# Splitting the opening's weights and norming its embeddings on another engine, and moving the S5 rotations' multiples

## The chip, the cores and the metric

The kernel runs on one core of a Trainium2 chip. The metric is the device time of one execution in microseconds (us), as the median of several runs. The core has five engines with instruction queues of their own: TensorE (PE, with its weight loads shown as PEld), VectorE (DVE), ScalarE (ACT), GpSimd (POOL) and SyncE (SP, which here only issues DMAs). Each engine works through its queue in order, and semaphores make one engine wait for another.

## The reference, cut to what matters

One decoder layer over 1024 tokens of width 1024, with a memory of 256 tokens:

```
h     = layer_norm(x); mem_n = layer_norm(mem)
z     = h @ w_in                        # columns: u (512) | q k | v | r (512) | gate rank 16
y_ssm = s5_mixer(u)                     # 32 groups x 16 channels, 64 complex states a group
y_gla = gla_mixer(q, k, v, r, gates)    # 4 heads, gated linear attention
h     = layer_norm(a*h + concat(y_ssm, y_gla) @ w_out)
h     = layer_norm(a*h + cross_attention(h, mem_n, w_mq, w_mkv, w_mo))
h     = layer_norm(a*h + relu(h @ w_ff1)**2 @ w_ff2)
```

In the S5 mixer each state obeys s[l] = A s[l-1] + (B u)[l] with a complex A = mag (cos + i sin) for each of the 2048 states, and y = Re(C s) + D u. The gate r enters as r * sigmoid(r).

## The kernel before, in words

**Products.** Everything is in float32. For a matmul that must keep that accuracy, each operand is *split* into a high part (rounded by ScalarE as it copies, `act(hi, src)`) and a low part (`lo = src - hi`, one tensor_tensor on VectorE or GpSimd, line 150); `mm3` then issues three matmuls (high x high, high x low, low x high, line 171). `weight` loads a raw block of 128x1024 into one of four `raw` buffers by SyncE's queue and splits it into one of five buffers (`hl`). Which engine makes the low part is given block by block by a bit mask: `eng(bits, i)` is VectorE where bit i is set, and GpSimd where it isn't. The masks that the change touches are `MO0` (the output weights `wo` of memory head 0), `MWR` (the four blocks `wr` of the gate r) and `MWU` (the four blocks `wu` of the S5 input u).

**The opening.** Memory is normed and head 0 of the cross-attention is folded into weights (`mem_stream`: its products with `kvT`, the split projection of the memory). Then the eight embedding tiles of 128 tokens follow. `embed(tk)` norms tile `tk` in place (`layer_norm`, tile `xs`), has TensorE transpose it (line 259), splits the transposed tile into `h0T`, and `z_block` multiplies the tile before it by `wr`; `r_epi` finishes the gate (tile `rt`). In `layer_norm` the tile's mean and variance come from VectorE (`bn_stats`, and a chain of one-element instructions on `tq`). Then there are two ways, chosen tile by tile by a bit of `LIGHT`:

```
if light:
    stt(V, xt[:, lo_], xt[:, lo_], mv[:, 0:1], rows[:, 0, lo_], ALU.subtract, ALU.mult)
    stt(V, tq[:, 3:4], mv[:, 0:1], -1.0, tq[:, 0:1], ALU.mult, ALU.mult)
    act(xt[:, hi_], xt[:, hi_], AF.Identity, scale=tq[:, 0:1], bias=tq[:, 3:4])
    tt(G, xt[:, hi_], xt[:, hi_], rows[:, 0, hi_], ALU.mult)
else:
    stt(V, xt, xt, mv[:, 0:1], rows[:, 0, :], ALU.subtract, ALU.mult)
    act(xt[:, hi_], xt[:, hi_], scale=tq[:, 0:1])
```

After either, VectorE scales and shifts the lower half and GpSimd adds the shift of the upper half. So in the light way VectorE handles only the lower 512 columns, and GpSimd has two passes over the upper ones. `LIGHT` = 191 makes all tiles but tile 6 light.

**S5's tables.** VectorE works out exp, sin and cos of the 2048 states' steps (tiles of 128x16 in `prm`), the powers 0 to 8 of A (`pw`, in `par`), and the *rotations' multiples* `E0` and `E1`: powers of exp(8i angle) from which a batch's rotations over 128 blocks of eight tokens are put together. Sixteen pairs of groups are handled in eight batches of two. `s5_t0(b)` builds a batch's tables by outer products on VectorE: `Vt` (C times the powers), the input weights `wtmp` (B times the powers), and the rotations `rot` (E0 times E1). `s5_t1` transposes the weights, `s5_t2` makes the taps `Mt` by way of a DMA, `s5_m1` loads the inputs, `s5_m2` runs the scan on the rotated products, and `s5_m3` makes the outputs.

**What sets the order.** The program traces its instructions in source order, and a planner lays out each engine's queue ahead of time from that order and its own estimates of when operands are ready; earlier source lines have priority among those ready. `behind(split_u)` opens a stretch of the source (closed by `order.close()`) whose VectorE instructions may not be issued ahead of `split_u`, the last VectorE split of `wu`. The rotations' multiples stand ahead of that stretch, while the rest of the tables, the masks of the GLA levels and the first `s5_t0` stand in it. After it, `z_stream` multiplies by `wu`, with the four decay gates (`gate`, tiles `gst`, stored by SyncE's queue, line 559) between its products, and later S5 batches are interleaved with the rest.

Of the kernel before, what the change touches and what calls it, by code (L numbers as in the profile page):

```python
# [9 lines left out]
I32 = mybir.dt.int32  # L10
U8 = mybir.dt.uint8
AF = mybir.ActivationFunctionType
ALU = mybir.AluOpType
# [4 lines left out]
P = 128  # L18
# [5 lines left out]
NJ = NG // 2  # L24
# [5 lines left out]
LEVELS = (1, 2, 4, 8, 16, 32, 64)  # L30
# [2 lines left out]
FA = 2.6  # L33
FB = 4
FT = 4
LIGHT = 191
MT = 64
ML = 15
GE = 2.6
GA = 8.0  # L40
MW = 3
MV0 = 3
MO0 = 2
MWR = 4
MWU = 7
MQK = 3
MVV = 11
MW1 = 3
# [33 lines left out]
def hybrid_layer(  # L82
# [9 lines left out]
    V = nc.vector  # L92
    A = nc.scalar
    G = nc.gpsimd
# [20 lines left out]
    const = ctx.enter_context(tc.tile_pool(name="const", bufs=1))  # L115
# [27 lines left out]
    def ts(e, o, i, s1, s2=None, op0=ALU.mult, op1=None):  # L143
        if s2 is None:
            e.tensor_scalar(out=o, in0=i, scalar1=s1, scalar2=None, op0=op0)
        else:
            e.tensor_scalar(out=o, in0=i, scalar1=s1, scalar2=s2, op0=op0, op1=op1)  # L147

    def tt(e, o, a, b, op):
        e.tensor_tensor(out=o, in0=a, in1=b, op=op)  # L150

    def stt(e, o, a, s, b, op0, op1):
        e.scalar_tensor_tensor(out=o, in0=a, scalar=s, in1=b, op0=op0, op1=op1)  # L153
# [28 lines left out]
    def rsqrt_n(y, v, eps, t):  # L182
# [5 lines left out]
        for _ in range(3):  # L188
# [7 lines left out]
                    pattern=[[-1, P]], channel_multiplier=1)  # L196

    def eng(bits, i):
        return V if bits >> i & 1 else G
# [67 lines left out]
    prm_s = slot("prm", [P, 4096])  # L267
# [20 lines left out]
    for b in range(4):  # L288
        z = (b + 1) % 3 * 512 + 512
        t = mrow[:, 0:2, :].rearrange("p a n -> p (a n)")[:, z:z + 512].rearrange("p (k m) -> p k m", k=2)  # L290
# [94 lines left out]
    def mem_stream(heads, tag, room=None):  # L385
        nxt = mem_load(heads[0])
        yield 0
        for h in heads:
# [7 lines left out]
            for r0 in range(0, D, 256):  # L396
                ps = bank("d", (P, 2, MEM))
                for c in range(2):
                    ck = r0 // P + c
                    for dk in range(2):  # L400
# [7 lines left out]
            wo = [weight(w_mo[h * 256:(h + 1) * 256, n * 512:(n + 1) * 512].rearrange("(k p) n -> p k n", p=P),  # L408
                         [P, 2, 512], eng(MO1 if room is None else MO0, n), None if room is None else room[:, n]) for n in range(2)]
            vT = yield from mem_proj(ws)  # L410
# [66 lines left out]
    def embed(tk):  # L477
        xt = xs[tk // 4][:, tk % 4, :]
        layer_norm(xt, rows, LIGHT >> tk & 1)
        transposes(lambda k: xt[:, k * P:(k + 1) * P],  # L480
# [29 lines left out]
    def pt(n=1):  # L510
        i = scr_n[0]
        scr_n[0] += n
        return scr[:, i, :] if n == 1 else scr[:, i:i + n, :]

    e = V
    prm = pt(6)
    lr, li, ls = prm[:, 0, :], prm[:, 2, :], prm[:, 4, :]
# [49 lines left out]
    def keep(*dims):  # L567
        n = 1
        for d in dims:
            n *= d  # L570
        o = par_n[0]
        par_n[0] += n
        names = "abcd"[:len(dims)]
        return par[:, o:o + n].rearrange("p (" + " ".join(names) + ") -> p " + " ".join(names),
                                         **dict(zip(names, dims)))
# [34 lines left out]
    def cmul(e, o_re, o_im, a_re, a_im, b_re, b_im, t):  # L610
        tt(e, o_re, a_re, b_re, ALU.mult)
        tt(e, t, a_im, b_im, ALU.mult)
        tt(e, o_re, o_re, t, ALU.subtract)
        tt(e, o_im, a_re, b_im, ALU.mult)
        tt(e, t, a_im, b_re, ALU.mult)
        tt(e, o_im, o_im, t, ALU.add)
# [5 lines left out]
    mag, mag1 = exp_parts(zre)  # L622

    kk, hh, x2, sn, cm1, cs = (pt() for _ in range(6))
# [24 lines left out]
    tw = pt(4)  # L649
# [4 lines left out]
    n = 1  # L654
    while n < 8:
        bc = [pw[:, r, n, :].unsqueeze(1).to_broadcast([P, n, NJ]) for r in range(2)]
# [1 line left out]
             pw[:, 0, 1:n + 1, :], pw[:, 1, 1:n + 1, :], bc[0], bc[1], tw[:, 0:n, :])  # L658
        n *= 2

    m8 = keep(NJ)
    tt(e, m8, mag, mag, ALU.mult)
    tt(e, m8, m8, m8, ALU.mult)
    tt(e, m8, m8, m8, ALU.mult)
    pr, pi_ = cs, sn
    for i in range(3):
        o = (pt(), pt())
        cmul(e, o[0], o[1], pr, pi_, pr, pi_, tw[:, 0, :])
        pr, pi_ = o
    E0 = keep(2, 16, NJ)  # L670
    E1 = keep(2, 8, NJ)
    te = pt(8)
    for Et, cnt in ((E0, 16), (E1, 8)):
        G.memset(Et[:, 0, 0, :], 1.0)
        G.memset(Et[:, 1, 0, :], 0.0)
        n = 1
        while n < cnt:
            bc = [z.unsqueeze(1).to_broadcast([P, n, NJ]) for z in (pr, pi_)]
            cmul(e, Et[:, 0, n:2 * n, :], Et[:, 1, n:2 * n, :], Et[:, 0, 0:n, :], Et[:, 1, 0:n, :],
                 bc[0], bc[1], te[:, 0:n, :])  # L680
            o = (pt(), pt())
            cmul(e, o[0], o[1], pr, pi_, pr, pi_, tw[:, 0, :])
            pr, pi_ = o
            n *= 2

    order = ExitStack()
    order.enter_context(behind(split_u))

# [21 lines left out]
         fim.unsqueeze(2).to_broadcast([P, NJ, SH]), b2[:, 2])  # L710


    mask = const.tile([P, 5, 64], U8, name="mask")
    mk = prm_s[:, 0:5 * P].rearrange("p (a t) -> p a t", a=5)
    ii, jj, xf, gt, ge = (mk[:, i, :] for i in range(5))
    ii, jj = ii.bitcast(I32), jj.bitcast(I32)
    G.iota(ii, pattern=[[1, P]], base=0, channel_multiplier=0)
    G.iota(jj, pattern=[[0, P]], base=0, channel_multiplier=1)
    tt(V, gt, ii, jj, ALU.is_gt)
    tt(V, ii, ii, jj, ALU.bitwise_xor)  # L720
    tt(V, xf, ii, gt, ALU.mult)

    def right(ap, s, two):
        return ap.rearrange("p (n w s) -> p n w s", w=2, s=s)[:, :, two, :]

    for li, s in enumerate(LEVELS[:5]):
        ts(V, ge, xf, float(s), op0=ALU.is_ge)
        stt(V, mask[:, li, :].rearrange("p (n s) -> p n s", s=s), right(xf, s, 1), float(2 * s),
            right(ge, s, 1), ALU.is_lt, ALU.mult)


    NB = 2

    class Batch:


        def __init__(self, bt):
            self.bt = bt
            sa = slot("s5", [P, 4096])

            def region(o, pat, **kw):
                n = 1
                for v in kw.values():
                    n *= v
                return sa[:, o:o + n].rearrange(pat, **kw)

            self.uT = region(0, "p (g c) -> p g c", g=2 * NB, c=P)
            self.Mt = region(512, "p (g j n) -> p g j n", j=NB, g=2, n=P)
            self.Wt = region(1024, "p (r j n) -> p r j n", r=2, j=NB, n=P)
            self.wtmp = region(1536, "p (r j n) -> p r j n", r=2, j=NB, n=P)  # L750
            self.S = region(1024, "p (r j c) -> p r j c", r=2, j=NB, c=P)
            self.rot = region(2048, "p (r j c) -> p r j c", r=2, j=NB, c=P)
            self.rs = region(2560, "p (r j c) -> p r j c", r=2, j=NB, c=P)
            self.Vt = region(3072, "p (r j t h) -> p r j t h", r=2, j=NB, t=9, h=SH)
            self.tmp = region(3648, "p (j c) -> p j c", j=NB, c=P)
            self.tmp9 = region(0, "p (r j t h) -> p r j t h", r=2, j=NB, t=9, h=SH)

    rows2 = [slice(0, 64), slice(64, 128)]


    def s5_t0(b):

        j0 = b.bt * NB
        js = slice(j0, j0 + NB)
        def outer(e, o, w, a, m, shape, signs):

            shape = [P] + shape
            for r in range(2):
                for q in range(2):
                    tt(e, (o, w)[r][:, q], a(q ^ r).to_broadcast(shape), m(r).to_broadcast(shape), ALU.mult)  # L770
            for q in range(2):
                if signs[q]:
                    tt(e, o[:, q], o[:, q], w[:, q], signs[q])
                else:
                    stt(e, o[:, q], o[:, q], -1.0, w[:, q], ALU.mult, ALU.subtract)


        outer(V, b.Vt, b.tmp9, lambda q: C2[:, q, js, :].unsqueeze(2),
              lambda r: pw[:, r, :, js].rearrange("p t j -> p j t").unsqueeze(3), [NB, 9, SH], (ALU.subtract, None))

        w_, t_ = (z.rearrange("p r j (t h) -> p r j t h", t=T) for z in (b.wtmp, b.rs))
        outer(V, w_, t_, lambda q: Bb[:, q, js, :].unsqueeze(2),
              lambda r: pw[:, r, 0:8, js].rearrange("p t j -> p j t")[:, :, ::-1].unsqueeze(3), [NB, T, SH],
              (ALU.subtract, ALU.add))

        w_, t_ = (z.rearrange("p r j (a b) -> p r j a b", a=8) for z in (b.rot, b.S))
        outer(eng(CM, b.bt), w_, t_, lambda q: E0[:, q, :, js].rearrange("p a j -> p j a").unsqueeze(2),
              lambda r: E1[:, r, :, js].rearrange("p a j -> p j a").unsqueeze(3), [NB, 8, 16], (ALU.subtract, ALU.add))

# [88 lines left out]
    bat = {}  # L878

    def s5(stage_, i):  # L880
        if i < NBT:
            if stage_ is s5_t0:
                bat[i] = Batch(i)
            stage_(bat[i])

    s5(s5_t0, 0)
    order.close()


    qk = slot("qk", [P, 4, SEQ])  # L890
# [79 lines left out]
    dc, o = {}, 0  # L970
    for s in LEVELS + (P,):
        w = 2 * SEQ // s
# [444 lines left out]
    for _ in range(2):  # L1417
        z = wp.tile([P, 2, 2, 512], F32R, tag="w", name="w1q")
# [271 lines left out]
    for k in range(6):  # L1690
        banks = [(m, 0, 512, bank(("ddds", "ssgg")[k % 2][m])) for m in range(4)]
        for gp in range(NP):
            s = k * NP + gp
# [19 lines left out]
    for ms in ((0, 1), (2,), (3,)):  # L1713
        parts = [(m, c, w) for m in ms for c, w in (((0, 256), (256, 256)) if m == 3 else ((0, 512),))]
        for part in ([parts] if len(ms) == 2 else [[z] for z in parts]):
            banks = [(m, c, w, bank("d")[:, 0:w]) for m, c, w in part]
            for gp in range(NP):
                s = 6 * NP + gp
# [4 lines left out]
            for m, c, w, po in banks:  # L1723
                r = res(4 + m)[:, c:c + w]
# [38 lines left out]
```

## Time and profile before

| | |
|---|---|
| median of 3 runs | 1375.15 us (1372.4 to 1378.64) |
| the profiled execution | 1375.71 us, its span 1373.9 us |
| granted TensorE clock, mean | 0.992 of full speed |
| busy: TensorE / VectorE / ScalarE / GpSimd | 1332.4 / 962.5 / 572.7 / 367.3 us |
| DMA | 199.82 MB, mean 145 GB/s |

The span runs from the first to the last instruction of the core. A row of the profile names start and duration (in a timeline), engine, line of the kernel, operation, what is written and read, the shape and how often; in brackets stands how long the engine had been idle before it, and what ended that. Where several equal instructions follow each other they are one row with a count. A busy share is a mean over stages with different limits, so the opening is read by itself.

### The profile page before, as it was taken

How to read it: one execution, taken by the hardware profiler on the slowest of the kernel's cores; microseconds unless marked ns; L12 is line 12 of the kernel's file. 1: busy time of each engine (PE TensorE's matmuls, PEld its weight loads, DVE VectorE, ACT ScalarE, POOL GpSimd, SP SyncE). 2: the span in 40 equal slices, each digit the busy share in tenths (PEclk: the TensorE clock that was granted, in tenths of full speed). 3: DMA queues.
4: the chain of work that ended last, by engine and by line, in shares of the span. 5: the costliest groups of instructions: out<-in, count | busy, mean ns of one | idle time of the engine just before them, and what ended most of it. 6: DMA issues, size and time to landing. Idle time of an engine off the chain costs nothing. (4 is left out here: it accounts for less than half of the span.)

```text
span 1373.9 us, 18798 instructions
## 1 busy us (share of the span) xinstructions
PE 1332.4 (97%) x6824; PEld 1106.7 (81%) x6824; DVE 962.5 (70%) x1751; ACT 572.7 (42%) x953; POOL 367.3 (27%) x269
## 2 busy tenths in 40 slices
PE   6789999999999999999999999999999999999997
PEld 6576788888998888888888788788887888888886
DVE  8999788756874379745379866665556576668784
ACT  4434433342554244333023754545456343344441
POOL 1552010211534123000013134343332243003353
PEclk9899999999999999999999999999999999999999
DMA  9832342543667120311112557644446994334432
GB/s 301 267 125 85 112 123 53 176 152 118 219 197 248 53 86 16 123 31 31 32 46 85 185 171 242 197 155 162 155 167 228 318 318 132 103 108 159 136 108 92
DMA packets 155514, 199.82 MB, mean 145 GB/s; under 512 B 16294, under 2 KB 86044, under 8 KB 155292
## 3 DMA queue, kind: packets, MB, share of 16 engines
q1 hardware_dynamic: 143536, 179.44, 40.1%
q10 hardware_dynamic: 11884, 19.17, 3.8%
q8 instruction: 54, 0.88, 0.3%
q14 instruction: 40, 0.33, 0.1%
HBM read 140.38 MB, written 58.20 MB: 145 GB/s over the span
## 5 line engine op out<-in xcount | busy, mean ns | idle before, releaser
L171 PE MATMUL ps_d<-xt,w1q 128*128 128x512 f32 x576 | 137.4, 389 | 0.7 <-DVE hid L150 0.7
L171 PEld LDWEIGHTS ps_d<-xt,w1q 128*128 128x128 f32 x576 | 108.1, 188 | 23.5 <-DVE hid L150 1.1
L171 PE MATMUL ps_s<-cell 128*128 128x512 f32 x432 | 113.0, 389 | 0.0
L171 PE MATMUL ps_d<-cell 128*128 128x512 f32 x432 | 106.0, 389 | 0.5 <-DVE hid L150 0.5
L150 POOL TENSOR_TENSOR R<-R,row 128x512 f32<-128x512 f32 x27 | 35.6, 1332 | 231.9 <-ACT R L156 225.3
L171 PEld LDWEIGHTS ps_d<-cell 128*128 128x128 f32 x432 | 81.0, 188 | 17.7 <-DVE hid L150 0.9
L171 PEld LDWEIGHTS ps_s<-cell 128*128 128x128 f32 x432 | 81.1, 188 | 16.8
L156 ACT ACTIVATE hl<-raw 128x1024 fp32r<-128x1024 f32 x62 | 65.2, 1059 | 68.9 <-PE ps_d L171 57.6
L171 PE MATMUL ps_d<-hl,y 128*128 128x512 f32 x384 | 92.6, 395 | 0.0
L171 PE MATMUL ps_g<-xb,w1q 128*128 128x512 f32 x384 | 92.1, 392 | 0.0
L171 PE MATMUL ps_d<-hl,h0T 128*128 128x512 f32 x384 | 91.0, 393 | 0.6 <-DVE h0T L150 0.6
L171 PE MATMUL ps_d<-h0T,hl 128*128 128x512 f32 x384 | 90.8, 393 | 0.8 <-DVE hl L150 0.8
L171 PE MATMUL ps_d<-hl,p 128*128 128x512 f32 x384 | 89.0, 391 | 0.0
L171 PEld LDWEIGHTS ps_d<-h0T,hl 128*128 128x128 f32 x384 | 71.1, 188 | 20.1 <-issue 2.2
L156 ACT ACTIVATE hid<-hid 128x512 f32<-128x512 f32 x112 | 70.8, 632 | 39.2 <-DVE hid L150 37.4
L150 DVE TENSOR_TENSOR hl<-raw,hl 128x1024 fp32r<-128x1024 f32 x53 | 70.3, 1339 | 21.8 <-ACT hl L156 21.3
L150 DVE TENSOR_TENSOR cell<-ha,cell 128x1024 fp32r<-128x1024 f32 x56 | 82.3, 1471 | 3.5 <-ACT cell L156 3.5
L171 PEld LDWEIGHTS ps_d<-hl,h0T 128*128 128x128 f32 x384 | 71.1, 188 | 16.2 <-DVE h0T L150 1.1
L171 PEld LDWEIGHTS ps_d<-hl,p 128*128 128x128 f32 x384 | 71.6, 188 | 14.6
L171 PEld LDWEIGHTS ps_g<-xb,w1q 128*128 128x128 f32 x384 | 71.5, 188 | 14.6
L171 PEld LDWEIGHTS ps_d<-hl,y 128*128 128x128 f32 x384 | 70.7, 188 | 14.6 <-issue 0.3
L156 ACT ACTIVATE w1q<-raw 128x512 fp32r<-128x512 f32 x80 | 50.1, 629 | 69.0 <-PE ps_d L171 27.3
(295 smaller groups left out, 2744.9 us busy)
## 6 DMA issues: line engine op xcount, KB each, us to landing
g_d<-hid SPq DMA_DIRECT2D x112, 256.0 KB
ha<-g_d SPq DMA_DIRECT2D x56, 512.0 KB
raw<-in_w_ff_dram SPq DMA_DIRECT2D x40, 512.0 KB
b<-in_w_ff_dram SPq DMA_DIRECT2D x32, 512.0 KB
raw<-in_w_mkv_dram SPq DMA_DIRECT2D x16, 512.0 KB
raw<-in_w_in_dram SPq DMA_DIRECT2D x16, 512.0 KB
wq<-in_w_mq_dram SPq DMA_DIRECT2D x8, 512.0 KB
xs<-in_x_dram SPq DMA_DIRECT2D x8, 512.0 KB
```

Source lines behind the costliest of these rows:

```text
L150: e.tensor_tensor(out=o, in0=a, in1=b, op=op)
L156: A.activation(out=o, in_=i, func=f, **kw)
L171: PE.matmul(o, lhs(i), rhs(j), start=first and n == 0, stop=last and n == 2, skip_group_check=more)
```

## The change

- `LIGHT` becomes 0: all eight embedding tiles take the other way of norming. VectorE subtracts the mean and multiplies by the gain over all 1024 columns, and GpSimd keeps one pass over the upper half.
- `MO0` 2 to 3, `MWR` 4 to 15, `MWU` 7 to 15: five low parts (one block of `wo`, three of `wr`, one of `wu`) go from GpSimd to VectorE. `split_u` is then the split of the last block of `wu`.
- The code that makes `m8`, `E0` and `E1` moves from ahead of the stretch behind `split_u` to its end, after the first `s5_t0`. The first batch's rotations are made after it, by a new function `s5_r0`; the later batches call it at the end of `s5_t0`. Its scratch moves from the place of the states `S` to a new region `rt`, which is the place of the taps `Mt`.
- The masks move behind `order.close()`.

```
-LIGHT = 191        -MO0 = 2     -MWR = 4      -MWU = 7
+LIGHT = 0          +MO0 = 3     +MWR = 15     +MWU = 15
...
-    m8 = keep(NJ)
-    tt(e, m8, mag, mag, ALU.mult)
...                                   # E0, E1: moved, see below
     order = ExitStack()
     order.enter_context(behind(split_u))
...
-    mask = const.tile([P, 5, 64], U8, name="mask")
...
+            self.rt = region(512, "p (r j c) -> p r j c", r=2, j=NB, c=P)
...
     def s5_t0(b):
...
-        w_, t_ = (z.rearrange("p r j (a b) -> p r j a b", a=8) for z in (b.rot, b.S))
+        if b.bt:
+            s5_r0(b)
+
+    def s5_r0(b):
+        js = slice(b.bt * NB, b.bt * NB + NB)
+        w_, t_ = (z.rearrange("p r j (a b) -> p r j a b", a=8) for z in (b.rot, b.rt))
         outer(eng(CM, b.bt), w_, t_, lambda q: E0[:, q, :, js].rearrange("p a j -> p j a").unsqueeze(2),
               lambda r: E1[:, r, :, js].rearrange("p a j -> p j a").unsqueeze(3), [NB, 8, 16], (ALU.subtract, ALU.add))
...
     s5(s5_t0, 0)
+    m8 = keep(NJ)
+    tt(e, m8, mag, mag, ALU.mult)
+    tt(e, m8, m8, m8, ALU.mult)
+    tt(e, m8, m8, m8, ALU.mult)
+    pr, pi_ = cs, sn
+    for i in range(3):
+        o = (pt(), pt())
+        cmul(e, o[0], o[1], pr, pi_, pr, pi_, tw[:, 0, :])
+        pr, pi_ = o
+    E0 = keep(2, 16, NJ)
+    E1 = keep(2, 8, NJ)
+    te = pt(8)
+    for Et, cnt in ((E0, 16), (E1, 8)):
+        G.memset(Et[:, 0, 0, :], 1.0)
+        G.memset(Et[:, 1, 0, :], 0.0)
+        n = 1
+        while n < cnt:
+            bc = [z.unsqueeze(1).to_broadcast([P, n, NJ]) for z in (pr, pi_)]
+            cmul(e, Et[:, 0, n:2 * n, :], Et[:, 1, n:2 * n, :], Et[:, 0, 0:n, :], Et[:, 1, 0:n, :],
+                 bc[0], bc[1], te[:, 0:n, :])
+            o = (pt(), pt())
+            cmul(e, o[0], o[1], pr, pi_, pr, pi_, tw[:, 0, :])
+            pr, pi_ = o
+            n *= 2
+    s5_r0(bat[0])
     order.close()
+    mask = const.tile([P, 5, 64], U8, name="mask")
...
```

`cmul` is six VectorE instructions.

More of the change, by code (lines that the diff above doesn't have):

```diff
@@ L35 @@
 FT = 4
-LIGHT = 191
+LIGHT = 0
 MT = 64
@@ L42 @@
 MV0 = 3
-MO0 = 2
-MWR = 4
-MWU = 7
+MO0 = 3
+MWR = 15
+MWU = 15
 MQK = 3
@@ L659, in hybrid_layer @@
         n *= 2
-    m8 = keep(NJ)
-    tt(e, m8, mag, mag, ALU.mult)
[L663 to L684, printed above, removed]
     order = ExitStack()
@@ L710, in hybrid_layer @@
          fim.unsqueeze(2).to_broadcast([P, NJ, SH]), b2[:, 2])
-    mask = const.tile([P, 5, 64], U8, name="mask")
[L714 to L729, printed above, removed]
     NB = 2
@@ L758, in hybrid_layer, with outer @@
     rows2 = [slice(0, 64), slice(64, 128)]
+    def outer(e, o, w, a, m, shape, signs):
+        shape = [P] + shape
+        for r in range(2):
+            for q in range(2):
+                tt(e, (o, w)[r][:, q], a(q ^ r).to_broadcast(shape), m(r).to_broadcast(shape), ALU.mult)
+        for q in range(2):
+            if signs[q]:
+                tt(e, o[:, q], o[:, q], w[:, q], signs[q])
+            else:
+                stt(e, o[:, q], o[:, q], -1.0, w[:, q], ALU.mult, ALU.subtract)
     def s5_t0(b):
@@ L764, in s5_t0 @@
         js = slice(j0, j0 + NB)
[L765 to L775, printed above, removed]
         outer(V, b.Vt, b.tmp9, lambda q: C2[:, q, js, :].unsqueeze(2),
@@ L886, in hybrid_layer, with right @@
     s5(s5_t0, 0)
-    order.close()
+    m8 = keep(NJ)
[23 more added lines that the diff above has]
+    s5_r0(bat[0])
+    order.close()
+    mask = const.tile([P, 5, 64], U8, name="mask")
+    mk = prm_s[:, 0:5 * P].rearrange("p (a t) -> p a t", a=5)
+    ii, jj, xf, gt, ge = (mk[:, i, :] for i in range(5))
+    ii, jj = ii.bitcast(I32), jj.bitcast(I32)
+    G.iota(ii, pattern=[[1, P]], base=0, channel_multiplier=0)
+    G.iota(jj, pattern=[[0, P]], base=0, channel_multiplier=1)
+    tt(V, gt, ii, jj, ALU.is_gt)
+    tt(V, ii, ii, jj, ALU.bitwise_xor)
+    tt(V, xf, ii, gt, ALU.mult)
+    def right(ap, s, two):
+        return ap.rearrange("p (n w s) -> p n w s", w=2, s=s)[:, :, two, :]
+    for li, s in enumerate(LEVELS[:5]):
+        ts(V, ge, xf, float(s), op0=ALU.is_ge)
+        stt(V, mask[:, li, :].rearrange("p (n s) -> p n s", s=s), right(xf, s, 1), float(2 * s),
+            right(ge, s, 1), ALU.is_lt, ALU.mult)
     qk = slot("qk", [P, 4, SEQ])
```

## The prediction

> **What bounds the kernel now.** I read the page first, then the table of stretches, then TensorE's waits in the opening, then each engine's order in time there.
>
> ```profile
> PE 1332.4 (97%) x6824; PEld 1106.7 (81%) x6824; DVE 962.5 (70%) x1751; ACT 572.7 (42%) x953; POOL 367.3 (27%) x269
> ```
>
> ```profile
> 0.00:122.50 122.50, 97.24 (x537) 78.67 (x537) 113.81 (x379) 50.68 (x81) 48.19 (x51) 0.96 0.60 203
> 122.50:314.00 191.50, 191.45 (x1094) 151.69 (x1094) 147.00 (x334) 76.38 (x126) 24.96 (x36) 1.00 0.41 127
> ```
>
> The columns of the stretches are: length, then busy time of PE, PEld, DVE, ACT and POOL, then granted clock, DMA share and GB/s. TensorE is idle for 1373.9 - 1332.4 = 41.5 us in all. 25.3 us of that (122.5 - 97.24) lies in the opening, which holds nearly all that the change touches, and 0.05 us in the next 191.5 us. So a microsecond that TensorE's queue gains by 122.5 us moves everything behind it by a microsecond, and more than the opening's waits can't be won. From 20 us on these are, by the chain of waits (total, times, longest):
>
> ```profile
> PE ps_d L171 <- DVE kvT L150: 5.3, 2, 5.0
> PE ps_s L259 <- POOL xs L150: 4.7, 4, 2.3
> PE ps_d L171 <- ACT kvT L156: 3.4, 1, 3.4
> PE ps_d L171 <- DVE hl L150: 0.8, 1, 0.8
> PE ps_d L171 <- DVE h0T L150: 0.6, 1, 0.6
> ```
>
> That is 14.8 us: two waits for the split of head 0's value projection (kvT), four for GpSimd's part of the embedding norm, one for a split of the S5 input weights (hl). VectorE is busy 113.81 of 122.5 us, so most of these are its queue being late. Part of this busy time is waiting:
>
> ```profile
> 30.14 2.40 POOL L150 TENSOR_TENSOR wo<-raw,wo 128x1024 fp32r<-128x1024 f32 x1 [23.71 <-ACT wo L156]
> 36.76 5.87 POOL L150 TENSOR_TENSOR hl<-raw,hl 128x1024 fp32r<-128x1024 f32 x2 [4.22 <-DMA prm<-in_w_gate_up_dram]
> ```
>
> ```profile
> 30.18 2.38 DVE L153 SCALAR_TENSOR_TENSOR tq<-tq 128x1 f32<-128x1 f32 x1
> ...
> 37.05 3.37 DVE L150 TENSOR_TENSOR wo<-raw,wo 128x1024 fp32r<-128x1024 f32 x1
> 40.34 2.32 DVE L153 SCALAR_TENSOR_TENSOR tq<-tq 128x1 f32<-128x1 f32 x1
> ```
>
> The instruction of one element per row at 30.18 ends at 32.56, when GpSimd's weight split (30.14 to 32.54) ends. The one at 40.34 ends at 42.66, with GpSimd's pair (36.76 to 42.63). A weight split by GpSimd takes 2.4 us and holds VectorE up for nearly as long. VectorE does one in 1.23 us:
>
> ```profile
> 27.45 1.23 DVE L150 TENSOR_TENSOR hl<-raw,hl 128x1024 fp32r<-128x1024 f32 x1 [1.45 <-ACT hl L156]
> ```
>
> **The change part by part.** *Five weight splits go to VectorE* (head 0's first output weight, three of the gate's, the last of S5's). Each adds 1.23 us, 6.2 us in all. Beside the stalls above stand these under the fourth and the fifth split:
>
> ```profile
> 55.48 2.46 DVE L145 TENSOR_SCALAR prm<-prm 128x16 f32<-128x16 f32 x2
> ...
> 117.88 4.56 DVE L150 TENSOR_TENSOR hl<-raw,hl 128x1024 fp32r<-128x1024 f32 x2
> ```
>
> The small instructions of the norms that no GpSimd pass meets:
>
> ```profile
> L153 DVE SCALAR_TENSOR_TENSOR tq<-mv,tq 128x1 f32<-128x1 f32 x7 | 1.0, 148 | 0.0
> ```
>
> At 0.15 us for such a one, 30.18 loses 2.2, 40.34 loses 2.2, 37.05 loses 3.37 - 1.23 = 2.1, 55.48 loses 2.2, and 117.88 loses 4.56 - 2.46 = 2.1: 10.8 us less. Of it 6.5 us less and, with three splits, 3.7 us more lie ahead of this:
>
> ```profile
> 45.67 0.68 DVE L150 TENSOR_TENSOR kvT<-ps_d,kvT 128x512 fp32r<-128x512 f32 x1
> ```
>
> The weight buffers are also let go earlier. SyncE holds a gate weight's load for the buffer of the split at 30.14 (3.4 us), and ScalarE then waits 0.69 us for that weight, directly ahead of its half of kvT:
>
> ```profile
> SPq L205 <- POOL wo L150: 3.4, 1, 3.4
> ```
>
> ```profile
> 38.31 1.06 ACT L156 ACTIVATE hl<-raw 128x1024 fp32r<-128x1024 f32 x1 [0.69 <-DMA raw<-in_w_in_dram]
> ```
>
> I take 0.6 us of that off the 3.4 us wait.
>
> *Seven embedding tiles go the other way of norming*: one VectorE pass over 1024 in place of a pass over 512 and a small one, and one GpSimd pass in place of two.
>
> ```profile
> L150 POOL TENSOR_TENSOR xs<-xs,row 128x512 f32<-128x512 f32 x15 | 22.9, 1529 | 7.4 <-ACT xs L156 6.8
> ```
>
> ```profile
> L153 DVE SCALAR_TENSOR_TENSOR tq<-tq 128x1 f32<-128x1 f32 x48 | 18.4, 402 | 0.2
> ...
> L153 DVE SCALAR_TENSOR_TENSOR xs<-xs,mv,row 128x1024 f32<-128x1024 f32 x1 | 1.3, 1267 | 0.0
> ```
>
> ```profile
> L153 DVE SCALAR_TENSOR_TENSOR xs<-xs,mv,row x8: 731/743/1729, 21.3 to 86.8; 128x512 f32<-128x512 f32 x7, 128x1024 f32<-128x1024 f32 x1
> ```
>
> VectorE pays 1.27 - 0.74 - 0.15 = 0.38 us a tile, 2.6 us in all (0.74 is the median of the eight, the last row). GpSimd loses 7 x 1.53 = 10.7 us. The 48 small instructions cost 18.4 us where 48 x 0.15 = 7.2 would do: 11.2 us of stalls, 4.4 of them the two under splits above. The passes over 512, 0.74 at the median and up to 1.73, add an estimated 3 us. So some 10 us lie under GpSimd's other work of 29 us (these 22.9 and the gate's products): a third. A third of 10.7 is 3.6 us, so VectorE gains 1.0 us net, and the way from ScalarE to TensorE gets one pass of 1.3 us shorter in each tile.
>
> What this is for TensorE: kvT comes 6.5 - 3.7 = 2.8 us earlier for the splits, less 3 x 0.38 for three longer norms, plus some 0.7 for GpSimd passes that held two instructions up between 42.6 and 45.6: 2.4 us. The wait for h0T (0.6) goes, since the stall at 55.48 goes. Of the four waits for GpSimd's embedding pass (4.7) I take 3.0 us; the bounds are none (VectorE stays full there) and all. The wait for hl (0.8) goes. Sum: 0.6 + 2.4 + 0.6 + 3.0 + 0.8 = 7.4 us.
>
> *The rotations' multiples move* behind the S5 weights' splits and the first batch's products. It is 105 small VectorE instructions (3 + 18 + 48 + 36, counted in the code), and four short GpSimd memsets; it issues no DMA.
>
> ```profile
> 98.08:117.88 19.80, 19.18 (x126) 1.00 0.14 52
> 117.88:156.80 38.92, 38.81 (x95) 1.00 0.41 136
> 156.80:164.50 7.70, 0.70 (x5) 1.00 0.22 80
> ```
>
> ```profile
> 164.58 1.29 DVE L150 TENSOR_TENSOR s<-ps_s,s 128x512 f32<-128x512 f32 x2
> ...
> 167.88 2.08 DVE L150 TENSOR_TENSOR s<-s 128x508 f32<-128x508 f32 x4
> ```
>
> ```profile
> 174.85 0.72 PE L864 MATMUL ps_s<-s 64*128 64x128 f32 x8
> ```
>
> Here the stretches give VectorE alone. Without five others (3.2 us) and two stalls (2.2) the first stretch has 121 small instructions in 13.8 us, 0.114 each: the move is 12.0 us. Now they fill time in which TensorE never waits. Afterwards they stand in a stretch that is full (38.81 of 38.92 us), followed by 7.0 us of slack. The last S5 split on VectorE now ends at 122.4. With its queue empty it could end 1.2 us after the ScalarE half, at about 119.5 on the same clock:
>
> ```profile
> 117.23 1.06 ACT L156 ACTIVATE hl<-raw 128x1024 fp32r<-128x1024 f32 x1 [0.30 <-PE ps_d L171]
> ```
>
>  From there 156.8 - 122.4 = 34.4 us plus 12.0 end at 165.9, 1.3 us past the start of batch 0's rotation at 164.58. That chain ends at 169.96, and TensorE takes its result at 174.85: 4.9 us of cover against 1.3, so I cost the move at nothing. If the cover is gone, each further microsecond is one of TensorE's. Queued behind the later VectorE work are the four gates, and in SyncE's queue the loads behind the gates' stores:
>
> ```profile
> SPq L559 <- DVE gst L150: 18.1, 3, 14.8
> ```
>
> SyncE already stands 14.8 us for the longest. The gates come 12.0 - 2.9 = 9.1 us later, and so does what SyncE issues behind them, the first batch's inputs; they feed the products ahead of 164.58, and I count on the same 5 us of cover. The first rotations' scratch moves from the states' place to the taps', so the taps' loads now wait for it, and ScalarE's copy of the batch's weights no longer does.
>
> The profiled execution took 1375.71 us around a span of 1373.9, the runs' median is 1375.15. 1375.7 - 7.4 = 1368.3, and against the median 1367.8: I say **1368**.
>
> **The clock, and a rule.** A halved clock costs more than the wait itself:
>
> ```profile
> 39.91 1.45 PE L171 MATMUL ps_d<-wo,kvT 128*128 128x512 f32 x4 [3.35 <-ACT kvT L156]
> 46.40 6.92 PE L171 MATMUL ps_d<-wo,kvT 128*128 128x512 f32 x20 [5.04 <-DVE kvT L150]
> ```
>
> ```profile
> 93.66 5.70 PE L171 MATMUL ps_d<-hl,h0T 128*128 128x512 f32 x24
> ```
>
> ```profile
> 40.00:42.00 2.00, 1.36 (x4) 0.67 0.26 38
> ```
>
> Twenty products take 6.92 us after the gaps and 20 x 0.238 = 4.75 at 93.66. A mean of 0.67 from 40 to 42 puts the drop near 40.7, ahead of the second gap: the first gap of 3.35 us was enough, and the change shortens it only to some 2.7. I leave these 2.2 us in. The Trainium skill, TensorE: Matmul & The Clock Gate, section "What's actually happening", says that the clock halves after an idle window of about 3.4 us and returns after as much sustained work. By that rule neither gap would halve it any more, and the sum would be 9.6 us in place of 7.4. The trace agrees within its resolution (halved after 3.35 us idle), but shows no gap of 2.7 us.
>
> **The rivals.** *More goes* (0.15): both kvT waits shrink to the chain behind them, and a gap below 3.35 us leaves the clock up: 7.4 + 2.2 for the clock, up to 2.6 more of kvT and 1.7 more of the embedding waits: 10 to 14 us, 1363. For it: TensorE goes on at 39.91 with ScalarE's half of kvT, so VectorE's could lie 5 us earlier. Against it: instructions are issued in an order laid down beforehand, and weight splits now stand ahead of it.
>
> *Less goes* (0.15): VectorE stays full from 60 to 96 us, the embedding waits stay and kvT wins 1 to 2 us: 2 to 4 us, 1372. For it: four splits (4.9 us) and the longer norms (2.6) add work before 96 us. The Trainium skill, SBUF — State Buffer, section "Who interferes with whom", says that whichever of the two engines starts first keeps the shared port for its whole instruction. By that, the longer norms would hold GpSimd's remaining passes up; the trace shows the other direction, in the rows at 30.14.
>
> *The move eats the gain* (0.08): with the split of 119.5 not won, batch 0 is 12.0 - 7.0 = 5.0 us late, and a next batch's products (about 6 us) put ahead of it cost the same again: 11 - 4.9 = 6 us of TensorE, 1374. Against it: 7 us of slack stand in the row.
>
> *Slower* (0.12): the stalls stay with VectorE, falling on GpSimd's remaining passes, while 4.9 + 2.6 = 7.5 us of work are added to its full queue before 96 us: up to 1383. It decides once less than 7.5 of the 12.3 us (8.7 + 3.6) of stalls go. Against it: the stalls end to within 0.03 us with the very instructions that leave.
>
> **How the numbers follow.** The forecast has 0.50, with 5 to 10 us (1365 to 1370.5). A difference of 0.5% is 6.9 us, about what a measurement of this kernel can tell from none; two thirds of the forecast's case lie beyond it. Faster: 0.33 + 0.15 = 0.48. Same: 0.17 + 0.15 + 0.08 = 0.40. Slower: 0.12. The range leaves out the slower case and the far half of the first rival: 1360 to 1377.
>
> **What would show it.** Right: no GpSimd weight split before 122 us, small VectorE instructions at 0.15 us in the norms, kvT's VectorE half before 43.5, waits for GpSimd's embedding pass under 2 us, TensorE's idle time up to its first S5 product down by 7 us, and no TensorE wait between that and batch 0's outputs. Wrong: VectorE's kvT at 45 or later, a TensorE wait for VectorE in the S5 batches, or idle time that comes back past the opening because all later work is ordered anew.

## The result and the profile after

Median 1367.14 us after, 1374.85 us for the kernel before on the same chip: ratio 0.9949, 95% interval 0.9931 to 0.9968. On two more chips, beside the experiments, the ratio was 0.9968 both times (0.9954 to 0.9982 and 0.995 to 0.9985). One of the nine executions of the kernel before took 7260.04 us, and the ratio is that of the others. So by the ratio the change makes the kernel 0.3 to 0.5% faster, 4 to 8 us. By the medians of the two other chips it is less: 1369.40 after beside 1372.13 us, and 1369.20 beside 1371.74, so 2.7 and 2.5 us. 1368 was forecast. The first profiled execution took 1365.14 us around a span of 1363.3.

The page of after, the waits of TensorE from 20 to 130 us (engine, line, what it waited for: total, times, longest), and two stretches (columns as in the prediction):

```profile
PE 1327.5 (97%) x6824; PEld 1103.8 (81%) x6824; DVE 955.7 (70%) x1749; ACT 572.2 (42%) x953; POOL 335.7 (25%) x257
```

```profile
PE ps_d L171 <- ACT bgate L156: 1.9, 1, 1.9
PE ps_d L171 <- ACT kvT L156: 1.6, 1, 1.6
PE ps_s L259 <- DVE tq L153: 1.4, 1, 1.4
PE ps_s L259 <- POOL xs L150: 1.0, 2, 0.6
PE ps_d L171 <- DVE h0T L150: 0.6, 1, 0.6
PE ps_d L171 <- DVE kvT L150: 0.2, 1, 0.2
```

```profile
0.00:115.00 115.00, 97.42 (x547) 78.95 (x548) 98.97 (x292) 49.59 (x80) 24.46 (x39) 1.00 0.67 227
115.00:306.00 191.00, 187.72 (x1083) 149.08 (x1082) 151.50 (x418) 76.83 (x128) 24.19 (x37) 1.00 0.39 120
```

The waits fell from 14.8 to 6.7 us and kvT's VectorE wait from 5.3 to 0.2. But TensorE is now idle for 3.3 us of the S5 batches (191.00 - 187.72), where it was idle for 0.05 us. Two places measure the opening and the S5 stretch apart: ScalarE's third copy of an S5 input (`us`, which waits for TensorE alone) and the first norm product of the GLA. Each pair is before, then after:

```profile
138.52 0.60 ACT L156 ACTIVATE us<-ps_d 128x512 f32<-128x512 f32 x1 [1.08 <-PE ps_d L171]
...
314.57 1.72 PE L1113 MATMUL ps_g<-ones,y1f 128*128 128x2 f32 x14 [0.46 <-DVE y1f L150]
```

```profile
128.12 0.60 ACT L156 ACTIVATE us<-ps_d 128x512 f32<-128x512 f32 x1 [1.08 <-PE ps_d L171]
...
306.93 1.72 PE L1120 MATMUL ps_g<-ones,y1f 128*128 128x2 f32 x14 [0.46 <-DVE y1f L150]
```

The opening gained 10.4 us, S5 gave 2.8 back (178.81 us between the two, where before has 176.05), and 7.6 are left. The other 3 us of the span's 10.6 lie behind the norm product. 1.7 us of them are clock: before has two pieces of 3.41 us at half clock there (at 317 and 426 us), and this profile of after has one. In the next two profiles of after only 1.3 and 0.6 of these 3 us come back.

In the opening VectorE's half of kvT starts 7.5 us earlier (45.67 before), and TensorE's 20 products behind it take 4.84 us where they took 6.92 at half clock. Then TensorE stands 1.9 us for ScalarE. The row names the tiny `bgate`; the copy of h0T ahead of it ends 0.05 us before TensorE goes on. Both are late because ScalarE's cast of the last gate weight is late:

```profile
35.92 2.36 DVE L150 TENSOR_TENSOR hl<-raw,hl 128x1024 fp32r<-128x1024 f32 x2
38.19 0.69 DVE L150 TENSOR_TENSOR kvT<-ps_d,kvT 128x512 fp32r<-128x512 f32 x1
```

```profile
38.12 1.20 PE L171 MATMUL ps_d<-wo,kvT 128*128 128x512 f32 x4 [1.60 <-ACT kvT L156]
...
39.62 4.84 PE L171 MATMUL ps_d<-wo,kvT 128*128 128x512 f32 x20
...
50.52 0.74 PE L171 MATMUL ps_d<-hl,h0T 128*128 128x512 f32 x2 [1.90 <-ACT bgate L156]
```

```profile
45.95 2.93 ACTq L425 DMA_DIRECT2D vw_d<-prm  x2
48.92 1.06 ACT L156 ACTIVATE hl<-raw 128x1024 fp32r<-128x1024 f32 x1 [3.83 <-DMA vw_d<-prm]
49.89 0.58 ACT L156 ACTIVATE h0T<-ps_s 128x512 fp32r<-128x512 f32 x1
50.36 0.16 ACT L156 ACTIVATE bgate<-ps_g 128x2 f32<-128x2 f32 x1
```

The cast does not wait for its weight. That block's load was issued at 36.91, and the trace has its last landing (the arrival of its last part) at 41.79. The cast stands behind two stores to `vw_d` that ScalarE issues (the first row). The second is issued at 48.55. It signals its landing on the semaphore that the load of a later weight block uses (issued by SyncE at 40.07), and ScalarE holds it until that load's last landing, at 48.48.

In S5, two waits stand in TensorE's row, and one long wait at the head of ScalarE's queue:

```profile
150.59 1.04 PE L771 MATMUL ps_g<-s,par 64*16 64x128 f32 x8 [2.22 <-ACT s L156]
...
155.11 0.65 PE L757 MATMUL ps_g<-ident,s 128*128 128x128 f32 x4 [1.03 <-DVE s L150]
```

```profile
149.15 0.41 ACT L156 ACTIVATE s<-par 128x256 f32<-128x256 f32 x1 [7.00 <-DVE mask L153]
149.47 0.58 ACT L156 ACTIVATE us<-ps_d 128x512 f32<-128x512 f32 x1
149.95 0.59 ACT L156 ACTIVATE s<-ps_g 128x512 f32<-128x512 f32 x1
```

The instruction at 149.15 spreads `m8` for the third S5 batch, whose tile takes the place of `prm`, where the masks have their scratch. VectorE makes the masks behind the first batch's rotations and between those of the second (142.5 to 149.1), and the copy of the first batch's transposed weights (149.95), with which TensorE's wait of 2.22 us ends, queues behind that one instruction.

TensorE's second wait ends with this row of VectorE:

```profile
149.16 1.57 DVE L150 TENSOR_TENSOR s<-par 128x288 f32<-128x288 f32 x4
...
154.89 0.39 DVE L150 TENSOR_TENSOR s<-ps_g,par 16x32 f32<-16x32 f32 x2
```

At 155.11 TensorE transposes the second batch's input weights, which VectorE had finished by 133.6. What it waits for is a place in `ps_g`: the first of the two additions to the first batch's taps, which read `ps_g`, ends 0.05 us before. These additions stand in VectorE's queue behind the third batch's tables, which begin at 149.16, behind the last mask.

### The profile page after: what moved, and what is told of

The parts are those of the page before. It is cut to its first block, busy times and chain, and to the rows that moved or that the text cites. A ratio compares the mean times of both kernels' runs of the same rounds, so it can differ in the third digit from the quotient of the medians.

```text
span 1363.3 us, 18773 instructions
## 1 busy us (share of the span) xinstructions
PE 1327.5 (97%) x6824; PEld 1103.8 (81%) x6824; DVE 955.7 (70%) x1749; ACT 572.2 (42%) x953; POOL 335.7 (25%) x257
## 5 line engine op out<-in xcount | busy, mean ns | idle before, releaser
L150 DVE TENSOR_TENSOR cell<-ha,cell 128x1024 fp32r<-128x1024 f32 x56 | 87.7, 1567 | 3.4 <-ACT cell L156 3.4
```

## The experiments

Theory A: GpSimd's weight splits hold VectorE up, and the move takes some 3 us back in S5. The rivals stand in the expectations. The table has, for each profile: when the third `us` copy starts; the us from there to the GLA's first norm product (S5); TensorE's waits from 20 to 130 us and from 130 to 310 us, summed; the time at half clock up to 310 us, worked out from the granted clock of stretches of 2 us, to within some 0.1 us; and the ratio to before with its interval. Each row but the ratio is of one profile. The three profiles of after, one and the same kernel, differ by 2.4 us in the third copy, and before has a single one, so smaller differences between two kernels in that column show nothing.

| kernel | third copy | S5 | waits, opening | waits, S5 | half clock | ratio |
|---|---|---|---|---|---|---|
| before | 138.5 | 176.1 | 14.8 | 0 | 10.2 | 1 |
| after | 128.1 | 178.8 | 6.7 | 3.7 | 0.2 | 0.9949 (0.9931-0.9968) |
| after_again | 128.4 | 178.3 | 3.8 | 3.2 | 7.6 | 0.9968 (0.9954-0.9982) |
| after_third | 130.5 | 178.6 | 7.3 | 2.1 | 6.8 | 0.9968 (0.9950-0.9985) |
| engines_only | 133.9 | 175.8 | 9.0 | 0.5 | 6.8 | 0.9976 (0.9958-0.9993) |
| splits_only | 135.2 | 176.3 | 11.5 | 0.2 | 6.8 | 0.9990 (0.9975-1.0005) |
| light_only | 137.8 | 175.8 | 11.9 | 0 | 10.3 | 0.9998 (0.9983-1.0013) |
| move_only | 135.8 | 181.9 | 13.4 | 3.1 | 13.6 | 1.0036 (1.0022-1.0051) |
| ghost_splits | 132.3 | 178.3 | 9.0 | 2.7 | 3.4 | 0.9987 (0.9970-1.0004) |
| masks_early | 130.6 | 178.9 | 5.5 | 3.0 | 10.2 | 0.9964 (0.9943-0.9986) |
| late_store | 128.9 | 180.4 | 6.3 | 2.6 | 10.2 | 0.9959 (0.9944-0.9974) |
| table_pool | 130.7 | 181.6 | 7.6 | 3.7 | 10.2 | 0.9995 (0.9979-1.0012) |
| masks_late | 127.3 | 182.0 | 4.9 | 3.5 | 10.2 | 1.0004 (0.9987-1.0020) |
| table_pool_late | 129.7 | 182.1 | 6.0 | 3.2 | 13.6 | 0.9986 (0.9969-1.0004) |

(In move_only the third copy is held up in ScalarE's queue; its place is the first copy, 122.36, plus the 13.43 us that lie between the two elsewhere. Three chips were used. The kernel before had a median of 1372.48 us beside engines_only, move_only, ghost_splits and masks_early, of 1372.13 beside after_again, splits_only, light_only and late_store, and of 1371.74 beside the other four.)

**The two halves.** engines_only is before with the new masks, move_only is after with the old ones:

```
engines_only, from before:  LIGHT 191 -> 0, MO0 2 -> 3, MWR 4 -> 15, MWU 7 -> 15
move_only, from after:      LIGHT 0 -> 191, MO0 3 -> 2, MWR 15 -> 4, MWU 15 -> 7
```

> The kernel before with the four masks alone changed (five weight splits and seven tiles' norms), the rotations' multiples and the GLA masks left where they were. Theory A (the engines' part wins 9 to 10 us by TensorE's first S5 product, and the move gives some 3 us of it back in the S5 batches): TensorE reaches its first S5 product 8 to 10 us earlier than before, no wait over 1 us follows up to 300 us, and the time is 8 to 11 us under the kernel before, 1 to 3 us under the changed kernel. Rival B (the move is what empties VectorE's queue and makes the gain): 2 to 5 us under the kernel before, and above the changed kernel.

> The changed kernel with the four masks set back, so that only the rotations' multiples and the GLA masks have moved. Theory A: the opening up to the first S5 product stays as before within 1 us (a gain of 0.8 us for the wait for the S5 weights' split), then two TensorE waits of together 2 to 3.5 us appear between 140 and 170 us: 1 to 3 us slower than the kernel before. Rival B (the move makes the gain): 3 to 6 us faster than the kernel before.

The move alone came as theory A said, somewhat worse: 4.9 us slower. The engines alone missed: 3.3 us were won, where 8 to 11 were expected, and by the profile 4.7 us in the opening. The kvT wait is gone, but this stands in its trace:

```profile
114.88 5.52 PE L171 MATMUL ps_d<-h0T,hl 128*128 128x512 f32 x16 [2.97 <-DVE hl L150]
```

With the rotations' multiples still ahead in VectorE's queue, the splits of S5's last weights are late, 2.97 us where before had 0.77 and after has none. The two halves multiply to 0.9976 x 1.0036 = 1.0012, and together they give 0.995 to 0.997: so they are worth more together. One reason is shown: the move takes away the wait for `hl` that the other engines bring. The other is in part a matter of the clock. In S5 move_only gives back 5.8 us (181.9 - 176.1), after 2.3 to 2.8:

```profile
159.10 1.88 PE L771 MATMUL ps_g<-s,par 64*16 64x128 f32 x8 [3.06 <-ACT s L156]
```

Here the wait is one of 3.06 us, and TensorE is at half clock for 6.8 us behind it, which loses 3.4. After has a wait of 1.7 to 2.2 us in its place and, in two profiles, one of 1.0 to 1.1 behind it. That it is the earlier opening that makes the difference is not shown.

**The engines' two parts.** From before, `MO0`, `MWR`, `MWU` alone (splits_only) and `LIGHT` alone (light_only).

> The kernel before with the five weight splits on VectorE alone: the embedding's shift stays on GpSimd, the rotations' multiples stay ahead. Theory A: the kvT wait of 5.3 us and the halved clock go (together 7 to 9 us in the opening), the embedding's GpSimd waits of some 4.5 us stay, the S5 weights' splits come 2 to 3 us late behind the rotations' multiples; first S5 product 4 to 7 us before that of before, time 2 to 5 us under before. Rival B (the embedding's passes, not the splits, hold VectorE up): kvT wait stays over 3 us, time within 1.5 us of before.

> The kernel before with the embedding's shift moved to VectorE alone. Theory A: the GpSimd waits on xs fall from 4.7 to some 1 to 2 us, the kvT wait (5.3) and the halved clock stay, since the weight splits stay on GpSimd; time 0 to 3 us under before. Rival B (the embedding's passes hold VectorE up): kvT wait falls under 2 us and the time is 4 to 8 us under before. Rival C (the shift's extra 0.38 us a tile on VectorE is on the path): 1 us or more over before.

Neither can be told from before. splits_only has the kvT wait gone (0.2 us) and no half clock there, as theory A wants, but the expected GpSimd waits of 4.2 us and late S5 splits of 2.5 us remain, and a wait of 2.9 us for h0T at 56.6 brings the half clock there instead: its third copy is 3.3 us early. light_only keeps a kvT wait of 2.2 us and 10.3 us of half clock, and its copy is 0.7 us early. Theory A had the kvT wait of 5.3 us stay, and rival B had it fall under 2: GpSimd's embedding passes have a part in it, but don't make it alone.

**Passes that serve nothing.** ghost_splits is after plus three subtractions of 128x1024 by GpSimd, into a place that nothing reads, where the weight splits were:

```
+            tt(G, mrow[:, 3, :].rearrange(...), h_, h_, ALU.subtract)
```

> The changed kernel with three GpSimd passes of a weight split's size added, over the high parts of head 0's first output weight and the gate's first two, written to a place that nobody reads; VectorE's work is the changed kernel's. Theory A (a GpSimd pass holds VectorE up): VectorE has instructions of 2 us and more beside each of the three, its half of kvT comes 3 to 6 us later than 38.2 us, TensorE waits for it, and the time is 2 to 7 us above the changed kernel. Rival E (the gain came from the shorter split on VectorE and the weight buffers let go earlier, not from the stalls): kvT within 1 us, the time within 1 us of the changed kernel.

```profile
36.51 5.24 POOL L150 TENSOR_TENSOR mrow<-hl 128x1024 f32<-128x1024 f32 x2 [3.88 <-ACT hl L156]
```

```profile
37.08 5.75 DVE L150 TENSOR_TENSOR hl<-raw,hl 128x1024 fp32r<-128x1024 f32 x2
42.75 0.68 DVE L150 TENSOR_TENSOR kvT<-ps_d,kvT 128x512 fp32r<-128x512 f32 x1
```

```profile
43.48 6.46 PE L171 MATMUL ps_d<-wo,kvT 128*128 128x512 f32 x20 [3.12 <-DVE kvT L150]
```

VectorE's work is that of after. Yet its two splits take 5.75 us where after's take 2.36, kvT starts 4.6 us later, TensorE waits 3.12 us and its 20 products run at half clock. That shows the mechanism: a GpSimd pass beside VectorE's instructions makes VectorE late, with VectorE's own work unchanged. The place was not the one in before to the microsecond, so the size is not that of before. In time, 0.9987 where after has 0.9949 to 0.9968, the intervals overlap, and no run of after stands beside it on that chip.

**Where the S5 time went.** masks_early has the masks ahead of the order stretch, in another scratch:

```
+    mk = cst.rearrange("p (a t) -> p a t", a=4)       # ahead of order = ExitStack()
-    mk = prm_s[:, 0:5 * P].rearrange("p (a t) -> p a t", a=5)
```

> The changed kernel with the GLA masks' instructions taken ahead of the stretch behind the last S5 split, in scratch of their own (the place of C, which is copied out before). Theory C (the last mask holds ScalarE's queue for 7.0 us, because the third S5 batch's tables take the place of the masks' scratch, and TensorE waits behind it): ScalarE's wait for the masks is gone, TensorE's waits of 2.2 and 1.0 us between 150 and 156 us fall under 1 us together, and the time is 2 to 3 us under the changed kernel. Rival D (the 12 us of rotations' multiples are themselves what is late): ScalarE waits as long for another VectorE instruction, and the time is within 1 us of the changed kernel.

ScalarE's wait for the masks went (it waits 4.41 us for another VectorE instruction, at 143.44, ahead of what TensorE needs). TensorE waited 2.14 us for the tap additions instead, which stand behind the third batch's tables here too (the first ends at 155.92); S5 stayed as long (178.9). So the masks alone were not what set the stretch, but the planner laid out both queues anew. Three kernels beside a third run of after took this further: table_pool lets GpSimd spread the third batch's `m8`, masks_late moves the masks' code behind the fourth batch, and table_pool_late does both.

```
table_pool:  -        act(tmp, m8b)
             +        G.tensor_copy(out=tmp, in_=m8b)      # in the third batch
masks_late:  +        mk = stage.tile([P, 4, P], F32, tag="rt", bufs=3, name="mk")
             +        if i == 3:
             +            masks()
```

> The changed kernel a third time, as the measure on this chip for the three kernels beside it. Theory A: no wait of VectorE on kvT over 0.5 us in the opening, TensorE's two S5 waits of some 2 and 1 us behind ScalarE and VectorE at 150 to 156 us again, the GLA's first norm product at 306 to 308 us; where the clock is halved in the opening may differ from the other two profiles. Time 4 to 8 us under before.

> The changed kernel with one instruction moved: the third S5 batch's copy of the multiples (128x256), which waited 7.0 us at the head of ScalarE's queue for the last mask, goes to GpSimd. Theory A (that wait holds up the copies of the first batch's products behind it): TensorE's wait of 2.2 us on ScalarE at 150.6 us is gone or under 0.5, the wait on VectorE's products at 155 grows by no more than 2 us, the S5 products end 1 to 2 us earlier against the first S5 product than in the changed kernel. Rival (VectorE alone, late by the rotations and masks, sets the stretch): the wait only changes its releaser, and the sum of the waits from 145 to 165 us stays at 3 to 3.5 us.

> The changed kernel with the masks' 13 VectorE instructions (6.6 us) moved behind the fourth S5 batch and their scratch to a staging tile, so they stand neither ahead of the S5 batches' products nor on the place that the third batch takes. Theory A: the sum of TensorE's S5 waits falls from 3.2 us to 1 to 2.2 us (VectorE's products, 2.1 in the kernel with early masks, may stay), nothing changes in the opening; time 1 to 2 us under the changed kernel, near the limit of what can be told. Rival (VectorE is full here whatever the masks do): waits sum 3 us or more and no gain.

> The changed kernel with both edits: masks behind the fourth S5 batch, the third batch's copy on GpSimd. Theory A: if ScalarE's queue and VectorE's products are the two causes of the 3.2 us, both waits are nearly gone (sum under 1 us), the GLA's first norm product comes 2 to 3 us earlier against the first S5 product than in the changed kernel, and the time is 2 to 3 us under it: the fastest of all. Rival: the sum stays over 2 us, since the rotations' 12 us themselves, on VectorE ahead of the batches, are what is late.

after_third repeats the ScalarE wait (1.70 us); the one for VectorE is gone there, and 3.4 us of half clock stand in its place. In table_pool ScalarE's wait is gone and the wait for VectorE is 3.66 us, all in one: the sum is 3.7 us, as in after. The rival is right, and Theory A's cause, ScalarE's queue, fell: VectorE sets the stretch, by the tap additions behind the third batch's tables. And S5 is 2.8 us longer than in after, with the same sum of waits. The stretches show why (length, busy times, then the granted clock third from the end):

```profile
157.62 0.39 DVE L150 TENSOR_TENSOR s<-ps_g,par 16x32 f32<-16x32 f32 x2
```

```profile
157.85 1.12 PE L757 MATMUL ps_g<-ident,s 128*128 128x128 f32 x4 [3.66 <-DVE s L150]
```

```profile
154.00:158.00 4.00, 0.34 (x2) 0.15 (x2) 3.97 (x12) 0.00 (x0) 0.35 (x2) 0.93 0.22 66
158.00:162.00 4.00, 4.00 (x21) 2.66 (x22) 1.45 (x5) 1.29 (x3) 0.00 (x0) 0.50 0.10 21
162.00:166.00 4.00, 4.00 (x14) 3.11 (x14) 3.87 (x8) 0.00 (x0) 0.00 (x0) 0.72 0.18 41
```

TensorE is at half clock from some 157.4 to 164.3, 6.8 us, which loses 3.4. In after the same idle time lies in two pieces, 2.22 and 1.03 us, and the clock stays at 1.00. masks_late goes the same way, with one wait of 3.05 us. Its masks are not late at all: behind the third batch's tables (144.5 to 152.1) the planner puts them from 152.0, still ahead of the first tap addition:

```profile
152.01 0.93 DVE L150 TENSOR_TENSOR mk<-mk 128x128 f32<-128x128 int32 x3
...
153.37 0.17 DVE L150 TENSOR_TENSOR s<-ps_g,par 16x32 f32<-16x32 f32 x1
```

table_pool_late keeps a wait of 3.15 us for the tap additions, where under 1 us in all was expected. None of the three beat after_third, and table_pool and masks_late (0.9995 and 1.0004 beside 0.9968) look slower. No kernel put the tap additions ahead of the third batch's tables; whether that would win the 2.3 to 2.8 us is open.

**ScalarE's wait in the opening.** late_store was made on the premise that the cast at 48.92 waits for the last gate weight's transfer. It issues each embedded tile's store one tile later:

```
-        nc.scalar.dma_start(out=h0_d[tk * P:(tk + 1) * P, :], in_=xt)
+        held.append(lambda: nc.scalar.dma_start(out=h0_d[tk * P:(tk + 1) * P, :], in_=xt))
```

> The changed kernel itself, once more, so that the kernels of this call stand beside it on one chip. Theory A (GpSimd's weight splits held up VectorE; the move of the rotations' multiples gives some 3 us back in S5): the profile repeats the first one, TensorE's longest waits from 20 to 130 us being 1.9 us on ScalarE and no VectorE wait on kvT over 0.5; time 7 to 8 us under before. If the waits come out otherwise (a kvT wait of over 2 us, a gate wait of none), then single profiles differ by as much as the parts that I compare, and only the times of several rounds decide.

> The changed kernel with each embedded tile's store to DRAM issued one tile later, so that the first one (512 KB, issued at 41.2 us) does not run while the last gate weight's 512 KB arrive. Theory A (that weight's load, crowded by stores, sets ScalarE's cast at 48.92 and so TensorE's wait of 1.9 us): the cast comes 1 to 2 us earlier, the wait at 50.5 falls under 0.9, the first S5 product comes about 1 us earlier, time 0 to 2 us under the changed kernel. Rival (the load was issued too late, because its buffer came free late, or small-packet loads delay it): the wait stays between 1.5 and 2.3 and the time within 1 us.

The edit did not do what it says: the planner issued the first store at the same time (41.19 us, 41.20 in after), and ScalarE's cast started at 48.90. So it tests nothing, and the premise does not hold either. In late_store the store to `vw_d` ahead of the cast is issued at 48.52, behind the landing at 48.45 of the load that shares its semaphore; in after_again the two stand at 48.73 and 48.66. Whether another order of loads or another semaphore would bring the cast forward was not tried. The time, 0.9959, is within the interval of after_again. That of after_again, 0.9968, is 4.4 us under before, where 7 to 8 were expected. What its profile shows is worth more: the first wait is that of after, but the clock isn't.

```profile
38.21 1.19 PE L171 MATMUL ps_d<-wo,kvT 128*128 128x512 f32 x4 [1.64 <-ACT kvT L156]
...
39.72 6.42 PE L171 MATMUL ps_d<-wo,kvT 128*128 128x512 f32 x20
...
50.70 0.73 PE L171 MATMUL ps_d<-hl,h0T 128*128 128x512 f32 x2 [0.41 <-ACT bgate L156]
```

```profile
38.00:46.00 8.00, 7.79 (x33) 6.03 (x34) 8.00 (x21) 3.78 (x9) 1.80 (x1) 0.79 0.89 296
52.00:60.00 8.00, 7.51 (x31) 6.03 (x32) 7.86 (x21) 3.69 (x7) 2.40 (x2) 0.79 0.93 286
```

The 20 products took 1.6 us longer at half clock, and the wait behind ScalarE's cast was 1.5 us shorter. TensorE went on at 50.70 in place of 50.52. Up to there ScalarE's store, and so the load's landing, is the bound, and what the clock wins or loses ahead of it is hidden.

## Why the prediction was right, point by point

**By two errors of opposite sign.** The sum said 7.4 us for the opening and nothing for S5. The profiles show 10.4, 10.2 and 8.1 us in the opening (three of after against the one of before) and 2.8, 2.3 and 2.6 us given back in S5. So that 1368 came close is in part luck; on the two other chips the ratio stands for 4.4 us, less than the 5 to 10 that were forecast.

*Splits and VectorE (right in kind, too small).* No GpSimd weight split stands ahead of 122 us, and ghost_splits shows what one costs. The term mis-sized is kvT: I took 2.4 us and the split moved by 7.5. The three moved splits that I put ahead of it are there (one of `wo` at 29.08, two of the gate at 35.92). What I missed is the order: in before four embedding tiles' norm passes stand ahead of kvT's split, the last at 44.10 (1.65 us); in after two do (21.43 and 30.36), and the third comes at 41.18. Not all 7.5 is TensorE's: ScalarE's late cast, behind its stores, takes a part.

*ScalarE's half of kvT.* 0.6 us taken, 1.8, 1.8 and 0.9 measured (waits of 1.6, 1.6 and 2.5 us after 3.4).

*Embedding.* 3.0 us taken. The GpSimd waits fell from 4.7 to 1.0 in all three profiles, but two have a new wait of 1.4 us for VectorE's norm chain: 2.3 to 3.7 us net. The wait for h0T (0.6) was to go and stayed. The one for hl (0.8) went, by the move: with the engines alone it grew to 2.97 us.

*The move (the step that failed).* I costed it at nothing, with 4.9 us of cover between batch 0's rotation and TensorE's use of it. The rotation was not the first thing that TensorE needed of VectorE's queue. The masks stand in it too, and ScalarE's queue waits for the last of them; so do the first batch's tap additions, behind the third batch's tables, and TensorE's transposes at 155 wait for them, ahead of batch 0's states. The masks' move had no cost in the sum at all. "No TensorE wait between that and batch 0's outputs" was wrong: 1.7 to 3.3 us, and in two profiles of three a part of it, 1.0 to 1.1 us, was the wait for VectorE in the S5 batches that the prediction had named as a sign of being wrong. What the prediction named as queued behind the longer stretch, the gates and SyncE's loads, cost nothing that the waits show.

*The clock.* I kept 2.2 us of half clock in, since a wait of some 2.7 us would remain and still halve it. The wait was 1.60, 1.64 and 2.46 us in the three profiles of after, and only that of 1.64 us was followed by half clock (the row of 38 to 46 us). The Trainium skill, TensorE: Matmul & The Clock Gate, section "What's actually happening", adds that the window of 3.4 us runs free of the kernel, so that the same kernel meets it at another phase in each run. The three profiles of after agree with that; they do not agree with the rule that a whole window must be idle, since 1.64 us was enough.

*The rivals.* "More goes" is what the opening did, and part of "the move eats the gain" is what S5 did. "Slower" did not come: most of the stalls went. Some remain under GpSimd's embedding passes: a one-element instruction lasts 1.26 us at 51.76, and a norm pass over 1024 columns 2.27 us at 69.95, where others take 1.28.

## What to carry to other kernels

When work is moved along a full queue, go through everything that queue feeds and find the first consumer on the bounding engine; the cover of the moved item itself proves nothing about its neighbours. Test parts of a change together as well as alone: here one half won 3.3 us and the other lost 4.9, and together they win 4 to 8, since one removed the other's new wait. Before blaming a transfer for an instruction's wait, look when it landed, and what stands ahead of the instruction in its own queue. And removing a wait may lose time, if what remains is one longer idle gap in place of two short ones.

## What the hardware showed that was not expected

Up to 310 us the time at half clock comes, within the rounding of the rows, in pieces of about 3.4 us: after_again has 2 x 8.00 x 0.21 = 3.4 us in each of its two stretches above, table_pool 6.8 in S5, before 10.2 up to 100 us. In after_again's trace the clock changes at 39.69, 43.10, 53.34 and 56.75 us: 3.41, 10.24 and 3.41 us apart, whole multiples of 3.41. Waits of 1.2 to 2.6 us were followed by half clock in some profiles and not in others; each of the four waits of 3.05 us or more that TensorE had in S5 was. A piece in which TensorE is the bound loses up to 1.7 us (half of 3.4), and with none to four of them up to 310 us, depending on the profile, this is part of the spread between executions of one kernel.

In this program a DMA's issue can hold up an engine until another DMA with the same semaphore has landed. In ten of the profiles ScalarE's last store to `vw_d` is issued 0.07 to 0.08 us behind the last landing of the load that used its semaphore before (after 48.48 and 48.55), and the cast behind it starts 0.4 us later; in after that is 7.1 us behind the landing of its own data.
